# The ffn of an encoder block as seven block products for eight, with two of four sums of weights made by adding transfers

## The chip, the cores and the metric

The kernel runs on one core of a Trainium2 chip. A core has five engines that run side by side and wait for each other through semaphores: TensorE (PE, matrix products; PEld is its loading of the stationary operand), VectorE (DVE), ScalarE (ACT), GpSimd (POOL) and SyncE (SP), which here only issues transfers. Sixteen DMA engines move data between the chip's memory (HBM, "DRAM" in the code) and the core's own memory SBUF; matrix products are summed in PSUM, eight banks of 128 x 512 float32. The metric is the device time of one execution in microseconds (us), the median of the runs. The time before is 1940.48 us (three runs, 1940.22 to 1940.63).

## The reference

One block for 512 tokens of width 2048, all in float32. A norm, one input projection, two kinds of token mixing side by side, an output projection with residual; then a dense feed-forward network (ffn) with residual, and a last norm. Cut to the lines that matter here:

```
h = rmsnorm(x, norm_mix)
z = h @ w_in                                  # 2048 -> 3072
y = concat(fourier_mixer(z[:, :1024]), gating_mixer(gelu(z[:, 1024:])))
x = x + y @ w_out                             # 2048 -> 2048
h2 = rmsnorm(x, norm_ffn)
x = x + (silu(h2 @ w_gate) * (h2 @ w_up)) @ w_down     # 2048 -> 5632 -> 2048
out = rmsnorm(x, norm_final)
```

The three products of the ffn are about three quarters of all multiplications.

## The kernel before, in words

**Products.** A float32 product is made of three passes in the format float32r: each operand is split exactly into a high part and a low part, and high x high, high x low and low x high are summed in PSUM (`mm3`, lines 80 to 84). Each operand must therefore be split first. `weights` (lines 66 to 78) loads a unit of weights of 128 x 1024 (512 KB) by SP, ScalarE casts it to the high part (line 76), VectorE subtracts to get the low part (line 77). Three buffers each hold raw, high and low units, so SP's loads run up to three units ahead and wait for the buffer of an older unit.

**Stages.** The first 478 us or so make the input's norm, the Fourier half, the gate's half and the output projection. In the output projection four columns blocks of 512 (`n`) are made one after the other, each in four banks, one for each tile of 128 tokens. Behind each block VectorE adds the residual into `x2`, ScalarE makes the sums of squares, and `transposes` (lines 439 to 449) turns the block round on TensorE and splits it into `h2`. The norm's factor by token isn't known yet at that point; it is applied later, to the results of gate and up.

**The ffn.** The hidden width 5632 is 44 tiles of 128. `gate_up(f)` (lines 486 to 500) makes one tile of gate and one of up: for each, 16 steps of 128 over the width 2048, three passes each, a stationary tile of weights of 128 x 128 and 512 columns of `h2` that stream through. Then come the norm's factor, the gating (by tanh) and the split of the result, `act`. `down` (lines 505 to 511) multiplies `act` with the units of the third matrix, 512 columns wide, for a group of 4 hidden tiles at a time (`GROUPS`), and VectorE adds the result from PSUM into `x2` (line 511). Gate and up run one tile ahead of down. Behind the last small group the last norm is made and stored by token tile (lines 530 to 554).

**Order.** SP's transfers go in the order in which the code writes them. The order on the other engines is made by a planner from the dependencies, the order of the code and its own costs for each instruction: it may put an instruction forward if an earlier one isn't ready by its reckoning. On the chip each engine then works through its list in that order.

Of the kernel before, what the change touches and what calls it, by code (L numbers as in the profile page):

```python
# [38 lines left out]
def encoder_block(ctx, tc, a, out):  # L39
    """The block on one core.  # L40

    A float32 product is carried by float32r passes: an operand is hi + lo exactly, hi its
    leading 12 bits and lo the other 12, and hi*hi + hi*lo + lo*hi is accumulated in float32.
    """
# [3 lines left out]
    # loads and stores in the order written here  # L48
# [3 lines left out]
    hpool = ctx.enter_context(tc.tile_pool(name="h", bufs=2 * KT))  # L52
    spool = ctx.enter_context(tc.tile_pool(name="s", bufs=24))
# [9 lines left out]
    def htile(name):  # L63
        return hpool.tile([P, S], F32R, tag="h", name=name)

    def weights(src, name, pieces=1):
        """A unit of weights, as hi and lo."""
        raw = wpool.tile([P, U], F32, tag="raw", name=f"raw_{name}")
# [11 lines left out]
    def mm3(ps, lhs, rhs, first, last):  # L80
        """ps += lhs.T @ rhs, both as (hi, lo)."""
# [8 lines left out]
    # the tensor engine's clock rises with its use: keep it at work until the first operands are there  # L90
# [9 lines left out]
    def rsqrt(dst, ssq, scale, shape, name):  # L100
        """dst = 1 / sqrt(ssq * scale + eps), with a Newton step."""
# [22 lines left out]
    def load_h(k):  # L124
# [4 lines left out]
        hi, lo = htile(f"hhi{k}"), htile(f"hlo{k}")  # L129
# [11 lines left out]
    def by_token(pss, units, nk, lhs, name, per_k=None, then=()):  # L141
        """Four banks, one for each token tile: sum over k of lhs(k).T @ the unit's columns.
# [294 lines left out]
    h2 = []  # L437

    def transposes(n):
        for i in range(4):  # L440
# [188 lines left out]
```

## Time and profile before

| what | before |
|---|---|
| median of three runs | 1940.48 us |
| profiled execution: its span, the only time of its own that the page gives | 1938.5 us |
| TensorE busy | 1919.9 us, 99% |
| VectorE, ScalarE, GpSimd busy | 45%, 28%, 6% |
| mean granted TensorE clock | 0.997 |
| transfers | 197.51 MB, mean 102 GB/s |

The profile is one execution, recorded on the chip. Its page gives the busy time of each engine; a chain of waits, followed back from the last instruction (it tells what set the end); and groups of equal instructions with the mean time of one. Further views are asked of the same trace: busy times in chosen stretches, the chain in order of time, single instructions. Rows of groups read: line of the code, engine, operation, result and operands, shapes, count; then busy time in us, mean ns of one; then idle time of the engine before them and what ended it. Matmuls overlap in the pipeline, so the time that one really takes is the step from one start in the chain to the next, not the mean of its group. Rows of stretches read: from and to, length, busy time of PE, PEld, DVE, ACT and POOL with their instruction counts, granted clock, busy share of the DMA engines, GB/s.

### The profile page before, as it was taken

What the parts mean: (1) busy time and instruction counts of PE and PEld (TensorE: products, weight loads), DVE (VectorE), ACT (ScalarE), POOL (GpSimd) and SP (SyncE); (2) the same over time, 40 slices, a digit from 0 to 9 for tenths busy, and PEclk for the clock granted to TensorE, in tenths of its full rate; (3) what the DMA queues carried; (4) which work ended last, traced back from release to release, by engine and by line L of the source; (5) the groups of instructions that cost most, each with busy time, mean ns of one, the idle gap of its engine ahead of it and who ended that gap; (6) DMA issues with size and microseconds to landing.
All of it is one profiled execution on the core that took longest, in us unless ns stands there. A gap on an engine that the chain in (4) does not pass through costs nothing.

```text
span 1938.5 us, 20697 instructions
## 1 busy us (share of the span) xinstructions
PE 1919.9 (99%) x8610; PEld 1593.7 (82%) x8610; DVE 866.2 (45%) x1006; ACT 544.1 (28%) x684; POOL 124.2 (6%) x96
## 2 busy tenths in 40 slices
PE   9999999999999999999999999999999999999996
PEld 8888888888888888888888888888888888888885
DVE  7555663333434334343444343443433433434447
ACT  6345532223322221222212222222222122222224
POOL 5001110000000000000000000000000000000003
PEclk9999999999999999999999999999999999999998
DMA  6223224423222323323233223232232232332332
GB/s 240 95 70 108 90 74 141 142 87 119 88 98 87 109 98 98 98 91 104 89 98 98 98 87 109 87 109 98 92 100 95 94 98 98 98 98 87 106 104 94
DMA packets 55965, 197.51 MB, mean 102 GB/s; under 512 B 6592, under 2 KB 6720, under 8 KB 55872
## 3 DMA queue, kind: packets, MB, share of 16 engines
q1 hardware_dynamic: 55584, 195.15, 30.2%
q8 instruction: 67, 1.10, 0.2%
q0 software_dynamic: 288, 1.05, 0.2%
q14 instruction: 26, 0.21, 0.0%
HBM read 191.98 MB, written 4.19 MB: 101 GB/s over the span
## 4 chain that ended last, share of the span: by engine, by line
PE 97%; DVE 1%; ACT 1%; DMA 0%; issue 0%; POOL 0%; SPq 0%; ACTq 0%; DVEq 0%
PE up L83 8%; PE g L82 8%; PE g L83 8%; PE up L82 8%; PE g L84 8%; PE up L84 8%; PE d L84 8%; PE d L83 8%; PE d L82 8%; PE o L84 3%; PE o L83 3%; PE o L82 3%; PE a L82 2%; PE a L83 2%; PE a L84 2%; PE v L82 1%
## 5 line engine op out<-in xcount | busy, mean ns | idle before, releaser
L82 PE MATMUL up<-h2hi,hi_up 128*128 128x512 f32 x704 | 274.0, 389 | 0.0
L83 PE MATMUL up<-h2lo,hi_up 128*128 128x512 f32 x704 | 273.9, 389 | 0.0
L82 PE MATMUL g<-h2hi,hi_g 128*128 128x512 f32 x704 | 273.9, 389 | 0.0
L84 PE MATMUL g<-h2hi,lo_g 128*128 128x512 f32 x704 | 273.9, 389 | 0.0
L83 PE MATMUL g<-h2lo,hi_g 128*128 128x512 f32 x704 | 273.9, 389 | 0.0
L84 PE MATMUL up<-h2hi,lo_up 128*128 128x512 f32 x704 | 273.9, 389 | 0.0
L82 PE MATMUL d<-hi_d,act 128*128 128x512 f32 x672 | 261.4, 389 | 0.0
L83 PE MATMUL d<-lo_d,act 128*128 128x512 f32 x672 | 261.4, 389 | 0.0
L84 PE MATMUL d<-hi_d,act 128*128 128x512 f32 x672 | 261.4, 389 | 0.0
L511 DVE TENSOR_TENSOR x<-d,x 128x512 f32<-128x512 f32 x192 | 131.4, 687 | 160.4 <-PE d L84 159.4
L77 DVE TENSOR_TENSOR lo_up<-raw_up,hi_up 128x1024 fp32r<-128x1024 f32 x88 | 141.7, 1610 | 127.8 <-ACT hi_up L76 127.8
L76 ACT CAST hi_g<-raw_g 128x1024 fp32r<-128x1024 f32 x88 | 92.8, 1054 | 367.8 <-PE g L83 144.7
L76 ACT CAST hi_d<-raw_d 128x1024 fp32r<-128x1024 f32 x84 | 88.6, 1055 | 382.2 <-PE d L84 242.8
L77 DVE TENSOR_TENSOR lo_g<-raw_g,hi_g 128x1024 fp32r<-128x1024 f32 x88 | 107.7, 1224 | 150.7 <-ACT hi_g L76 150.6
L76 ACT CAST hi_up<-raw_up 128x1024 fp32r<-128x1024 f32 x88 | 92.8, 1054 | 272.2 <-PE up L83 140.4
L77 DVE TENSOR_TENSOR lo_d<-raw_d,hi_d 128x1024 fp32r<-128x1024 f32 x84 | 114.5, 1363 | 97.3 <-ACT hi_d L76 97.3
L84 PEld LDWEIGHTS g<-h2hi,lo_g 128*128 128x128 f32 x704 | 132.1, 188 | 27.5
L82 PEld LDWEIGHTS up<-h2hi,hi_up 128*128 128x128 f32 x704 | 132.1, 188 | 27.5
L82 PEld LDWEIGHTS g<-h2hi,hi_g 128*128 128x128 f32 x704 | 132.1, 188 | 27.4
L84 PEld LDWEIGHTS up<-h2hi,lo_up 128*128 128x128 f32 x704 | 132.1, 188 | 27.4
L83 PEld LDWEIGHTS g<-h2lo,hi_g 128*128 128x128 f32 x704 | 132.1, 188 | 27.4
L83 PEld LDWEIGHTS up<-h2lo,hi_up 128*128 128x128 f32 x704 | 132.1, 188 | 27.3
(229 smaller groups left out, 2511.6 us busy)
## 6 DMA issues: line engine op xcount, KB each, us to landing
raw_g<-in_w_gate SPq DMA_DIRECT2D x88, 512.0 KB, 3.3
raw_up<-in_w_up SPq DMA_DIRECT2D x88, 512.0 KB, 3.3
raw_d<-in_w_down SPq DMA_DIRECT2D x84, 512.0 KB, 3.3
raw_o<-in_w_out SPq DMA_DIRECT2D x32, 512.0 KB, 3.3
raw_v<-in_w_v SPq DMA_DIRECT2D x16, 512.0 KB, 3.3
raw_u<-in_w_u SPq DMA_DIRECT2D x16, 512.0 KB, 3.4
raw_a<-in_w_a SPq DMA_DIRECT2D x15, 512.0 KB, 3.5
x<-in_x SPq DMA_DIRECT2D x8, 512.0 KB, 8.0
```

Of the source, the lines that this page charges most:

```text
L76: nc.scalar.copy(hi[:, c], raw[:, c])
L77: nc.vector.tensor_sub(lo[:, c], raw[:, c], hi[:, c])
L82: mm(ps, lhs[0], rhs[0], start=first, stop=False)
L83: mm(ps, lhs[0], rhs[1], start=False, stop=False)
L84: mm(ps, lhs[1], rhs[0], start=False, stop=last)
L511: nc.vector.tensor_add(x2c(m, n), ps, x2c(m, n))
```

## The change

Strassen's scheme (in Winograd's form) makes a product of two matrices, each cut into 2 x 2 blocks, from 7 products of blocks in place of 8, with sums of blocks before and after. The change applies it once to each product of the ffn.

**Gate and up.** A block is two hidden tiles (`p` of 22) of one matrix. The seven forms of the normalised, transposed input (`hs`, four blocks and sums of them, halves of 256 tokens) are made and split once, ahead of all of them, by `ffn_input`. The norm's factor must be in the input now, so the transposes move from the output projection to behind the finished norm. Each of the seven products of a block (`product` in `matrix`) takes one unit of weights or of sums of weights, and makes 8 steps of three matmuls, 256 columns wide. Products 1 and 2 share a bank, 5 and 3 too; VectorE and ScalarE put the four results together.

**Weights.** Five raw units are loaded for a block. Two of them are sums of two quarters of the matrix: the first quarter by SP as before, the second by a transfer from GpSimd's queue that adds to what is in SBUF (`accum_op`). Two further sums are made by VectorE in `form`. Loads are written four products ahead (`LEAD`).

**Order and storage.** All of gate and up comes first. The activations, their sums and both parts of each are written to DRAM (`ad`, 512 KB a store, four for each pair of blocks, from GpSimd's queue) and are read back for down, one form of a chunk of four hidden tiles at a time. The residual goes to DRAM (`xd`) and comes back as the start of down's sums.

**Down.** Two blocks of columns (`np_`) for each group of one or two chunks; each product has `size` x 12 matmuls, 512 columns wide, in two banks; VectorE adds them into six sums, `acc`, which the last group puts together.

The buffers: `hpool` is gone, `spool` has 43 slots of 512 KB for 24, the three high and low buffers stay.

```
-GROUPS = [4] * 10 + [2, 2]
+GROUPS = [2, 2, 2, 2, 2, 1]
+FORMS = 7
...
+            if n % 2:
+                nc.gpsimd.dma_start(xd[m, n // 2], x2[m][n // 2])
...
+    ORDER = (1, 5, 2, 6, 7, 3, 4)
+        LOADS = ((1, 0, (0,)), (5, 1, (0, 1)), (2, 2, (2,)), (3, 3, (3,)), (7, 4, (3, 1)))
...
+    def load_raw(r, i, srcs, name):
+        r[i] = slot(f"raw{i}_{name}")
+        nc.sync.dma_start(r[i], srcs[0])
+        for more in srcs[1:]:
+            nc.gpsimd.dma_start(r[i], more, accum_op=ALU.add)
...
+    def form(r, i, name):
...
+        elif i == 6:
+            nc.vector.tensor_add(r[5], r[5], r[3])
+        w = split_weights(r[5] if i in (6, 4) else r[i], f"{name}_{i}")
+        if i == 6:
+            nc.vector.tensor_add(r[5], r[5], r[2])
+        return w
...
+    def combine(t, A11, A12, A21, A22):
+        nc.vector.tensor_sub(t[0], A21, A22)
+        nc.vector.tensor_sub(t[1], t[0], A11)
+        nc.vector.tensor_add(t[2], t[1], A12)
+        nc.vector.tensor_sub(t[3], A11, A21)
+
+    def ffn_input(n):
+        xn = [slot(f"xn{n}_{i}", F32, (P, 2, S)) for i in range(2)]
+        for m in range(NT):
+            nc.vector.tensor_scalar_mul(xn[m // 2][:, m % 2, :], x2c(m, n), rstd2[:, m : m + 1])
+        r = [slot(f"h2_{n}_{i}", F32, (P, 2, S)) for i in range(2)]
+        for i in range(4):
...
+            for m in range(NT):
+                nc.tensor.transpose(ps[:, m * P : (m + 1) * P], xn[m // 2][:, m % 2, i * P : (i + 1) * P], ident)
+            nc.scalar.mul(r[i // 2][:, i % 2, :], ps, g_ffn[:, c : c + 1])
...
+        combine(t, A11, A12, A21, A22)
+        for i, s in ((1, A11), (5, t[0]), (2, A12), (6, t[1]), (7, t[3]), (3, t[2]), (4, A22)):
+            x = slot(f"hs{n}_{i}", F32R, (P, 2, 2, H))
+            nc.scalar.copy(x[:, :, 0, :], s)
+            nc.vector.tensor_sub(x[:, :, 1, :], s, x[:, :, 0, :])
+            hs[n][i] = x
...
+        def product(i, into, first=True):
+            step()
+            hi, lo = form(r, i, name)
...
+            for j in range(KT // 2):
+                x = hs[j // 2][i][:, j % 2]
...
+                mm(b, lo[:, c], x[:, 0, :], start=first and j == 0, stop=False, skip_group_check=True)
...
+                    mm(b, hi[:, c], x[:, 1, :], start=False, stop=False, skip_group_check=True)
+                    mm(b, hi[:, c], x[:, 0, :], start=False, stop=last, skip_group_check=True)
+            return b
+        A = product(1, "A")
+        nc.scalar.copy(m1, A)
+        E5 = product(5, "D")
+        A = product(2, "A", False)
+        nc.scalar.copy(o[:, 0, 0, :], A)
+        B = product(6, "B")
+        nc.vector.tensor_add(u, B, m1)
+        C = product(7, "C")
+        nc.vector.tensor_add(w, C, u)
+        nc.vector.tensor_sub(o[:, 1, 1, :], E5, w)
+        E5 = product(3, "D", False)
+        nc.vector.tensor_sub(o[:, 1, 0, :], E5, u)
+        E = product(4, "E")
+        nc.vector.tensor_add(o[:, 0, 1, :], E, w)
+        return o
...
+    def activation(p, g, u):
+        s = slot(f"s{p}", F32, (P, 2, 2, H))
+        nc.scalar.activation(s, g, AF.Tanh, scale=0.5)
+        nc.vector.scalar_tensor_tensor(s, s, 1.0, g, op0=ALU.add, op1=ALU.mult)
+        nc.vector.scalar_tensor_tensor(s, s, 0.5, u, op0=ALU.mult, op1=ALU.mult)
+        t = slot(f"at{p}", F32, (P, 4, H))
+        combine([t[:, i, :] for i in range(4)], s[:, 0, 0, :], s[:, 1, 0, :], s[:, 0, 1, :], s[:, 1, 1, :])
+        to = ad[p // 2].rearrange("f p r l h -> p f r l h")
+        for i, src in enumerate((s.rearrange("p a b c -> p (a b) c"), t)):
...
+            nc.scalar.copy(hi, src)
+            nc.vector.tensor_sub(lo, src, hi)
+            nc.gpsimd.dma_start(to[:, 4 * i : 4 * i + 4, p % 2, 0, :].bitcast(F32), hi.bitcast(F32))
+            nc.gpsimd.dma_start(to[:, 4 * i : 4 * i + 4, p % 2, 1, :].bitcast(F32), lo.bitcast(F32))
...
+    LEAD = 4
...
+    def step():
+        for args in wanted.pop(steps[0] + LEAD, ()):
+            load_raw(*args)
+        steps[0] += 1
...
+    def load_acts(i, chunk, size):
+        for c in range(chunk, chunk + size):
+            t = acts[c, i] = slot(f"a{c}_{i}", F32R, (P, 2, 2, H))
+            nc.sync.dma_start(t.bitcast(F32), ad[c, PLACE[i]].bitcast(F32))
...
+    def down(b):
...
+        def product(i, into, begin=True):
+            step()
...
+            for q in range(size):
+                hi, lo = form(r[q], i, f"{name}_{q}")
...
+                        mm(ps[into][t], xh, hi[:, c], start=start, stop=False, skip_group_check=True)
+                        mm(ps[into][t], xh, lo[:, c], start=False, stop=False, skip_group_check=True)
+                        mm(ps[into][t], xl, hi[:, c], start=False, stop=stop, skip_group_check=True)
+            if np_ == 1 and gi + 1 < len(GROUPS):
+                load_acts(i, chunk + size, GROUPS[gi + 1])
...
+        add("u", product(1, "A"), first)
+        add(22, product(5, "D"))
+        add(11, product(2, "A", False))
...
```

What is left out of the matmuls' loops in `down` runs over two halves of the chunk and two token tiles of 128. In the last group `down` also puts the sums together and squares them; the last norm's scaling of 16 tiles and the stores follow behind all of it.

More of the change, by code (lines that the diff above doesn't have):

```diff
@@ L427, in encoder_block @@
     x2 = [[slot(f"x2_{m}_{i}") for i in range(2)] for m in range(NT)]
+    xd = dram.tile([NT, 2, P, U], F32, name="xd")
     def load_x(i):
@@ L465, in encoder_block @@
     rsqrt(rstd2, xs, 1.0 / D, [P, NT], "ffn")
[L466 to L477 removed]
+    hs = [dict() for _ in range(4)]
@@ L530, in encoder_block @@
-    for n in range(4):
-        raw = wpool.tile([P, U], F32, tag="raw", name=f"raw_l{n}")
-        nc.sync.dma_start(raw, a["w_down"][f0 // 2][n])
-        p = pair(f"dl{n}")
-        split(raw, p)
-        units.append([p])
-    for m in range(NT):
-        o = [slot(f"o{m}_{i}") for i in range(2)]
-        oc = [o[n // 2][:, (n % 2) * S : (n % 2 + 1) * S] for n in range(4)]
-        for n in range(4):
-            down(f0, size, m, n, units[n], bank(f"d{f0}_{m}_{n}"))
-            squares(m, n, fss[:, m, n : n + 1])
-            last = m == NT - 1 and n == 3
-            (nc.vector if last else nc.gpsimd).tensor_tensor(
-                out=oc[n], in0=x2c(m, n), in1=gB[n // 2][:, (n % 2) * S : (n % 2 + 1) * S], op=ALU.mult
-            )
+    acts = {}
@@ L546, in encoder_block @@
+    for i in ORDER:
+        load_acts(i, 0, GROUPS[0])
+    for b in range(2 * FP, len(blocks)):
+        _, _, (gi, chunk, size, np_) = blocks[b]
+        down(b)
+        if np_ == 0 and gi == len(GROUPS) - 1:
+            for i in range(2):
+                nc.sync.dma_start(gB[i], a["norm_final"][:, i * U : (i + 1) * U].partition_broadcast(P))
+    for m in (0, 1, 2, 3):
+        half, t = m // 2, m % 2
         r = fr[:, m : m + 1]
```

231 lines of the change are left out of this document (150 added, 81 removed).

## The prediction

> **What bounds the kernel now.** I read the page's busy times first, then the chain of waits, then the busy times by stretches, then single rows for the price of each operation.
>
> ```profile
> span 1938.5 us, 20697 instructions
> PE 1919.9 (99%) x8610; PEld 1593.7 (82%) x8610; DVE 866.2 (45%) x1006; ACT 544.1 (28%) x684; POOL 124.2 (6%) x96
> PE 97%; DVE 1%; ACT 1%; DMA 0%; issue 0%; POOL 0%; SPq 0%; ACTq 0%; DVEq 0%
> 485.60:1923.00 1437.40, 1437.25 (x6344) 1189.71 (x6342) 613.76 (x662) 343.82 (x388) 71.58 (x56) 1.00 0.29 96
> 12.00:22.00 10.00, 10.00 (x46) 8.29 (x45) 10.00 (x7) 9.46 (x15) 9.61 (x6) 1.00 0.98 378
> 1903.59 0.23 PE d L84
> ...
> 1910.16 0.23 PE d L83
> ```
>
> TensorE is the bound: 97% of the chain, and through the ffn (485.6 to 1923) it is never idle, at full clock, with DVE 43% busy and the DMA engines at 0.29. Only fewer or shorter matmuls can help, while everything else has half its time to spare. The last row of stretches (columns: PE, PEld, DVE, ACT, POOL, clock, DMA share, GB/s) is the start, where transfers queue: full DMA engines carry 378 GB/s here. The two chain rows are 29 steps of the 128x512 matmul apart: 6.57/29 = 0.2266 us each; the 6336 of the ffn make 1436 us.
>
> **What it removes.** Seven block products for eight. Down goes from 2112 matmuls of 512 columns to 1848, at 0.2266: 478.6 to 418.8, so 60 us less. Gate and up go from 4224 of 512 columns (957.2 us) to 44 blocks x 7 products x 24 = 7392 of 256 columns. Their price stands in the Fourier stage:
>
> ```profile
> 119.06 0.12 PE dft L82
> ...
> 119.77 0.06 PE dft L82
> 119.83 0.12 PE dft L83
> ...
> 120.39 0.17 PE E L82
> ```
>
> The six matmuls from 119.06 to 119.77 are 256 wide: 0.1183 each. The five from 119.83 to 120.39 are 128 wide: 0.112, so there is a floor just below, where the load of weights sets the pace. I take 0.1185: 7392 x 0.1185 = 876 us, a gain of 81 and not the 120 of an eighth. A product then lasts 2.84 us, a block 19.9, 44 blocks 876. Bounds: 0.1170 and 0.125, 865 to 924.
>
> **The head.** Now three of the four transposes (1.88 us each) stand between output products, and TensorE goes from the fourth straight into the gate. After the change all wait for the finished norm, then for normalising, transposing, sums and splits of seven forms.
>
> ```profile
> 483.68 1.88 PE xt L444 x16
> 490.84 0.16 DVE L115 TENSOR_SCALAR rstd<-rsq_ffn 128x4 f32<-128x4 f32 x1
> L204 DVE TENSOR_SCALAR a0a<-a0a,rstd 128x512 f32<-128x512 f32 x2 | 0.9, 482 | 0.0
> L459 DVE TENSOR_TENSOR x<-o,x 128x512 f32<-128x512 f32 x16 | 10.9, 692 | 4.4 <-PE o L84 4.4
> ```
>
> The output products end at 483.7 - 3 x 1.88 = 478.0. The norm is ready 491.0 - 483.7 = 7.3 later: 485.3. Then VectorE does, for each of four column groups, 4 scalings of 0.482, 4 sums and 7 low parts of 512 elements at 0.692: 9.5, in all 38.2 us. Product 1 needs the fourth group's first form, behind which six low parts (4.2) are left: 519.3. TensorE can by then have done three quarters of products 1 and 5 (4.3 us, their banks are separate), so gate and up begin, in effect, at 515.0. If the planner takes one form of all groups first, some 8 us earlier (507); if TensorE does nothing meanwhile, 519.
>
> **VectorE's load.**
>
> ```profile
> L77 DVE TENSOR_TENSOR lo_g<-raw_g,hi_g 128x1024 fp32r<-128x1024 f32 x88 | 107.7, 1224 | 150.7 <-ACT hi_g L76 150.6
> L376 DVE SCALAR_TENSOR_TENSOR vn_lo<-v,vr,vn_hi 128x1024 fp32r<-128x1024 f32 x4 | 5.0, 1279 | 1.2 <-ACT vn_hi L375 1.2
> L511 DVE TENSOR_TENSOR x<-d,x 128x512 f32<-128x512 f32 x192 | 131.4, 687 | 160.4 <-PE d L84 159.4
> L253 DVE TENSOR_TENSOR ey<-ey,O 128x128 f32<-128x128 f32 x16 | 6.1, 379 | 0.0
> L76 ACT CAST hi_g<-raw_g 128x1024 fp32r<-128x1024 f32 x88 | 92.8, 1054 | 367.8 <-PE g L83 144.7
> ```
>
> A gate or up block: 7 low parts and 2 sums of weights at 1.224 (11.0); 5 sums from PSUM, 256 wide, not in the trace, between 0.379 (128 wide) and 0.687 (512), by the line through 0.69 and 1.22 nearer the lower: 0.43 to 0.48 (2.3); half an activation, which is two combined operations of 1.279, four sums of 0.43 and two low parts, 6.7 (3.4). Together 16.7 of 19.9 us: 84% busy, beside work that TensorE hides. A down block of two chunks lasts 7 x 24 x 0.2266 = 38.1 and gives VectorE 18 x 1.224 + 14 x 0.687 = 31.6, 83%. ScalarE has 7 casts of 1.054, two small copies and half an activation, under 10 of 19.9. VectorE has cover, but little.
>
> **Waits that it adds.** Each is bounded from nothing (covered) to its full length; all 57 us of them are estimates.
> - In a gate or up block product 3 adds into bank D, which product 5 filled and which `o[1,1]` must read first, behind `w`, behind product 7. Two 256-wide sums, 0.9, and up to a split of 1.2 ahead of them: 0 to 2.1 a block, 0 to 92. Product 4 has its own bank and can cover it if the planner puts it forward. It does such things:
>
> ```profile
> 496.47 0.44 PE rstd2B L475 x4
> 496.91 0.24 PE up L82
> 497.15 0.64 PE rstd2B L475 x4
> ```
>
> Here four broadcasts stood ready, four did not, and an up product was put between, though the code writes all eight first. I take 0.5 a block, 22.
> - Behind each pair of blocks VectorE has sum, combination, four sums and two low parts, 5.9 us, and the two products split ahead (three buffers) last 5.7; the next split is late by 0 to 2.0. I take 1.0 x 22 = 22. The activation's four stores queue on POOL ahead of the adding transfers of the next block, which so wait for it too.
> - Last group, one chunk: VectorE has 9 x 1.224 + 14 x 0.687 + 4 x 1.224 = 25.5 a block, TensorE 19.0: 0 to 13 over the two, I take 8.
> - Down's first product waits behind the residual's 4.2 MB and the first form's activations (1.0 MB) on SP's queue, which need slots that the last up block frees: 5.2 MB at 378 GB/s is 13.8. I take 5, of 0 to 14.
>
> **The tail.**
>
> ```profile
> 1922.46 0.39 PE L84 MATMUL d<-dl_hi,act 128*128 128x512 f32 x1
> 1930.57 0.16 DVE L547 TENSOR_REDUCE fs<-fss 128x1 f32<-128x4 f32 x1
> ...
> 1931.88 0.15 DVE L115 TENSOR_SCALAR fr<-rsq_fin 128x1 f32<-128x1 f32 x1
> L389 DVE SCALAR_TENSOR_TENSOR v<-sv,g_sgu,bB 128x512 f32<-128x512 f32 x8 | 5.9, 747 | 2.2 <-PE sv L84 2.2
> out_dram<-o SPq DMA_DIRECT2D x16, 256.0 KB, 2.8
> ```
>
> Now 1938.5 - 1922.9 = 15.6. After: two sums and a square (2.2), four token tiles at 1.46 for the norm and 4 x 0.747 = 3.0 for the scaling (17.8; no tile has all its squares before the last block), issue and landing (3.4): 23, of which a tile's start fits under the last product: 22.
>
> **The sum**, against the execution's own span: 515 + 876 + 419 + 22 = 1832, with the waits' 57 1889. The page gives the profiled execution no time but its span; the median of the runs, 1940.48, is 2.0 above it. So 1891.
>
> **The transfers.** Gate and up read 7 units of 512 KB a block for 4 and write 2 units of activations: 4.72 MB in 19.9 us, 237 GB/s. Down reads, in two blocks, 28 units of weights and 14 of activations: 22.0 MB in 76.2 us, 289 GB/s. Both are under 378, so I cost them at nothing: the cover is the spare third of the DMA engines.
>
> ```profile
> raw_g<-in_w_gate SPq DMA_DIRECT2D x88, 512.0 KB, 3.3
> wsp<-in_w_spatial POOLq DMA_DIRECT2D x1, 512.0 KB, 4.0
> L306 POOL DMA_DIRECT2D wsp<-in_w_spatial x1 | 0.7, 720 | 0.0
> L77 DVE TENSOR_TENSOR lo_up<-raw_up,hi_up x88: 1212/1225/2302, 484.9 to 1863.9; 128x1024 fp32r<-128x1024 f32 x88
> ```
>
> But two of the seven add to what lies in SBUF, and no transfer here adds. Say one occupies the engines like m plain ones: m = 1 from below (a plain POOL load lands in 4.0 against SP's 3.3), m = 4 from above if it were as far off as 4.0 x 4. At 1.387 us a unit a block needs (7 + 2m) units, a down pair 34 + 8m. I take m under 2.6, where both still fit. The Trainium skill ("Collectives: The Full Stack", "The bandwidth ceiling: the fold count and why AG ≠ RS ≠ AR") says that an adding transfer is slower because it reads two sources, about half the rate of a copy. That would be m = 2, a down pair at 69 of 76 us, and the sum as it is; no run here shows it.
>
> Other edits at nothing: the residual's 8 stores of 512 KB on POOL's queue fall where POOL has no arithmetic (the output products), the final norm's weights, now loaded a block before the end, are wanted only in the tail, and 22 x 4 activation stores are in the 2 units a block. If that cover were gone, a store costs its unit, 1.387 us.
>
> **Rivals.**
> - **The adding transfers pace it** (slower): with m = 4 a block needs 15 x 1.387 = 20.8 us for 19.9 (+40 over 44), a down pair 91.6 for 76.2 (+85 over 5.5). With half the waits (they fall under these) 1832 + 28 + 125 + 2 = 1987. It decides against the change from m of about 3.7. For it: lead of four products, 11.4 us, must hold a load, the adding and the split, 3.3 + 4.0 + 2.3 at idle queues. Against: spare a third, and a factor of 4 has no row. 0.21.
> - **VectorE paces it.** The last row quoted shows a split of 1.2 us held up to 2.3 when POOL works. If the four POOL transfers a block hold it for 0.72 each, 16.7 + 2.9 = 19.6, and 0.1 at each of 16 hand-overs makes 21.2: 44 x 1.3 = 57 in place of the first two waits' 44, so 1904; with down likewise near its 38.1, up to 1925. POOL computes nothing more in the ffn, which speaks against. The Trainium skill ("SBUF — State Buffer", "Who interferes with whom") says a VectorE operation with two SBUF inputs collides with POOL's reads, and infers that making descriptors needs the write side only; by that this rival falls. 0.18.
> - **The planner hides nearly all**: waits near 10 and the head at 507: 1836. 0.13.
> - **It isn't fewer cycles**: 256-wide matmuls in a long stream cost 0.1295, where gate and up gain nothing (957 / 7392): 1891 + 81 = 1972. The rows have six in a row, hardly slower than half. 0.04.
>
> **How the numbers follow.** Forecast 0.44, its own range 1850 to 1925. Low 1835 is the planner's case, high 1990 the adding transfers'. Under 0.2% (3.9 us) a measurement of this kernel tells nothing. Faster: 0.44 + 0.13 + 0.17 = 0.74; slower: 0.20 + 0.03 + 0.01 = 0.24; same 0.02.
>
> **What would show it.** TensorE at 0.1185 per 256-wide matmul; from the last output product to steady gate work some 37 us; a gate block of about 21 us, with the gap ahead of product 3 and behind each up block; down blocks near 38.5; a tail of 22. Wrong if the gaps end on raw tiles (transfers, m), if VectorE shows above 95% in gate and up, or if product 3's gap is over 1 us.

## The result, and the profile after

The changed kernel takes 2317.7 us (median of four runs, 2313.7 to 2321.7), the kernel before 1940.35 us beside it (1940.0 to 1940.6). The ratio is 1.1945, with a 95% interval of 1.1928 to 1.1962: 377 us slower, where 1891 us, 49 us faster, was predicted, and outside the predicted range. The profiled execution spans 2317.6 us against the predicted 1889.

The page of the changed kernel: span, busy times, granted clock in 40 slices, transfers of GpSimd's queue (q0), and the chain by engine and by line.

```profile
span 2317.6 us, 28514 instructions
PE 1929.6 (83%) x11506; PEld 1741.3 (75%) x11506; DVE 1304.8 (56%) x1577; ACT 799.7 (35%) x976; POOL 236.0 (10%) x265
PEclk9997788899979988888898899888888889999998
q0 software_dynamic: 33120, 120.60, 21.8%
PE 55%; DMA 11%; DVE 9%; issue 4%; ACT 3%; POOL 2%; POOLq 0%; DVEq 0%; ACTq 0%; SPq 0%
```

TensorE, 97% of the chain before, is 55% of it. No other engine took its place as the bound: VectorE is at 56%, the transfers at 11% of the chain. The kernel waits, now here and now there, and the clock falls with it. Where it waits is told by the busy times in stretches (columns as before: PE, PEld, VectorE, ScalarE, GpSimd, clock, DMA share, GB/s):

```profile
106.00:206.00 100.00, 76.88 (x377) 62.96 (x375) 38.99 (x98) 36.42 (x62) 6.26 (x6) 0.88 0.24 75
206.00:300.00 94.00, 60.81 (x231) 47.69 (x232) 36.20 (x42) 33.26 (x45) 6.48 (x5) 0.78 0.12 37
300.00:484.00 184.00, 140.22 (x583) 111.15 (x582) 54.03 (x66) 34.47 (x43) 8.85 (x7) 0.87 0.36 130
665.80:1850.60 1184.80, 975.27 (x7394) 965.71 (x7392) 682.48 (x792) 410.13 (x469) 143.47 (x173) 0.89 0.62 180
1852.50:2295.00 442.50, 427.04 (x1848) 349.97 (x1848) 342.55 (x368) 172.11 (x181) 39.27 (x46) 0.98 0.84 267
```

The first three rows lie ahead of the ffn, where no product was changed, and TensorE stands idle a quarter of the time there. The fourth is gate and up: 210 us idle, and a clock of 0.89. The last is down, 16 us above the predicted 427. The waits of TensorE that cost most (total, times, longest):

```profile
PE C_gate L559 <- DVE lo_gate L481: 149.9, 22, 10.1
PE u L82 <- ACT hi_u L76: 62.9, 8, 21.3
PE B_gate L559 <- DVE lo_gate L481: 59.6, 21, 3.0
PE xt L525 <- DVE xn L519: 30.2, 4, 8.2
PE v L82 <- ACT hi_v L76: 25.0, 3, 15.4
```

Set against the terms of the prediction, with the repaired kernel of the last experiment (called the repaired head there) beside it; each number is the distance between single rows of TensorE's timeline:

| term | predicted | changed kernel | repaired head |
|---|---|---|---|
| output products end at | 478.0 | 621.1 | 479.0 |
| from there to the first gate matmul | 37 | 44.7 | 23.3 |
| gate and up | 876 + 44 of waits | 1184.8 | 911.6 |
| gap ahead of down | 5 | 1.9 | 2.3 |
| down | 419 + 8 | 442.6 | 447.3 |
| tail | 22 | 22.5 | 23.5 |
| span | 1889 | 2317.6 | 1887.0 |

Of the 429 us missed, 143 lie ahead of the ffn, 8 in the head (from the output products to the first gate matmul), 265 in gate and up, 16 in down; the gap ahead of down was 3 shorter.

**What each gap waits for.** Ahead of the ffn TensorE waits for casts of `u` and `v`, and these for loads. Before, SP's queue waited there almost only for the split that empties one of the kernel's own three raw buffers (`SPq L73 <- DVE lo_o L77: 155.2, 30, 6.9`, and likewise for the other matrices; no wait for an operation of the mixing is above 5.9 us). In the changed kernel the loads of the same units wait for slots that other work holds:

```profile
SPq L73 <- ACT vt L365: 83.6, 5, 51.9
SPq L73 <- DVE yg L171: 62.2, 4, 39.7
```

The diff turned the three raw buffers and the 32 halves for `h` into ordinary slots of one pool of 43. A weight unit that was loaded into a buffer of its own now waits for a slot of a result of the gating half.

In gate and up, one pair of blocks lasts some 54 us. GpSimd's timeline around one of the gaps ahead of `C_gate` (product 7 of gate):

```profile
1200.79 0.80 POOL L598 DMA_DIRECT2D ad<-ahi  x1 [28.82 <-ACT ahi L596]
1204.45 0.79 POOL L599 DMA_DIRECT2D ad<-alo  x1 [2.86 <-DVE alo L597]
1205.23 0.75 POOL L598 DMA_DIRECT2D ad<-ahi  x1
1206.72 0.75 POOL L599 DMA_DIRECT2D ad<-alo  x1 [0.74 <-DVE alo L597]
1207.46 0.96 POOL L475 DMA_DIRECT2D raw_gate<-in_w_gate  x1
```

The adding transfer for product 7 waits for nothing of its own. Its plain load was issued by SP at 1187.69 and had long landed (the loads of gate take 12.8 us at most); the adding transfer stands behind four stores that wait for the activation, 28.8 us for the first of them. From there the chain in order of time:

```profile
1207.46 10.24 DMA raw_gate<-in_w_gate
...
1217.78 1.05 ACT hi_gate L480
...
1218.86 1.24 DVE lo_gate L481
...
1220.14 0.58 PE C_gate L559
...
1223.50 0.21 PE C_gate L564
...
1223.92 0.15 PE C_gate L563
...
1224.18 0.12 PE C_gate L559
```

Landing takes 10.2 us, with the DMA engines full meanwhile (a share of 1.05 from 1212.9 to 1220.1, against 0.62 on average in gate and up), then cast and split, and only then product 7. After an idle time of 7.3 us its first 17 matmuls take 3.8 us, most of them 0.21 each and not 0.12: the granted clock is 0.50 from 1220.2 to 1223.7 and 1.00 from 1224 on. That is a second cost of the same gap. Over all of gate and up it comes to 88 us: TensorE is busy for 975.3 us, and 7392 matmuls at 0.12 would be 887. By the steps, 54 of it follow gaps ahead of product 7 and 33 gaps ahead of product 6 (`B_gate`).

### The profile page after: what moved, and what is told of

It reads as the page before. It is cut to its first block, busy times and chain, and to the rows that moved or that the text cites. A ratio compares the mean times of both kernels' runs of the same rounds, so it can differ in the third digit from the quotient of the medians.

```text
span 2317.6 us, 28514 instructions
## 1 busy us (share of the span) xinstructions
PE 1929.6 (83%) x11506; PEld 1741.3 (75%) x11506; DVE 1304.8 (56%) x1577; ACT 799.7 (35%) x976; POOL 236.0 (10%) x265
## 3 DMA queue, kind: packets, MB, share of 16 engines
q0 software_dynamic: 33120, 120.60, 21.8%
## 4 chain that ended last, share of the span: by engine, by line
PE 55%; DMA 11%; DVE 9%; issue 4%; ACT 3%; POOL 2%; POOLq 0%; DVEq 0%; ACTq 0%; SPq 0%
DMA raw_gate<-in_w_gate 9%; PE o L82 2%; PE o L83 2%; PE o L84 2%; DVE lo_gate L481 2%; ACT hi_gate L480 2%; PE D_up L559 2%; PE C_gate L559 2%; PE D_up L564 2%; PE A_up L564 2%; PE A_up L559 2%; PE A_up L563 2%; PE D_up L563 2%; PE A_d L691 2%; PE A_d L692 2%
## 5 line engine op out<-in xcount | busy, mean ns | idle before, releaser
L480 ACT CAST hi_gate<-raw_gate 128x1024 fp32r<-128x1024 f32 x154 | 154.9, 1044 | 298.9 <-DMA raw_gate<-in_w_gate 140.4
L481 DVE TENSOR_TENSOR lo_gate<-raw_gate,hi_gate 128x1024 fp32r<-128x1024 f32 x154 | 184.1, 1219 | 122.2 <-ACT hi_gate L480 122.2
L481 DVE TENSOR_TENSOR lo_up<-raw_up,hi_up 128x1024 fp32r<-128x1024 f32 x154 | 188.5, 1224 | 101.6 <-ACT hi_up L480 101.2
L559 PE MATMUL C_gate<-hs,lo_gate 128*128 128x256 f32 x176 | 73.7, 419 | 149.9 <-DVE lo_gate L481 149.9
L559 PE MATMUL A_gate<-hs,lo_gate 128*128 128x256 f32 x352 | 111.3, 316 | 0.0
L82 PE MATMUL u<-h,hi_u 128*128 128x512 f32 x128 | 58.8, 459 | 62.9 <-ACT hi_u L76 62.9
L563 PE MATMUL A_gate<-hs,hi_gate 128*128 128x256 f32 x352 | 110.5, 314 | 0.0
L564 PE MATMUL A_gate<-hs,hi_gate 128*128 128x256 f32 x352 | 109.9, 312 | 0.0
L559 PE MATMUL B_gate<-hs,lo_gate 128*128 128x256 f32 x176 | 54.9, 312 | 59.6 <-DVE lo_gate L481 59.6
L77 DVE TENSOR_TENSOR lo_o<-raw_o,hi_o 128x1024 fp32r<-128x1024 f32 x32 | 39.0, 1224 | 112.5 <-ACT hi_o L76 112.5
L559 PE MATMUL D_up<-hs,lo_up 128*128 128x256 f32 x352 | 101.5, 288 | 0.0
L559 PE MATMUL D_gate<-hs,lo_gate 128*128 128x256 f32 x352 | 100.2, 285 | 0.0
L564 PE MATMUL A_up<-hs,hi_up 128*128 128x256 f32 x352 | 99.6, 283 | 0.0
L559 PE MATMUL A_up<-hs,lo_up 128*128 128x256 f32 x352 | 99.6, 283 | 0.0
L563 PE MATMUL A_up<-hs,hi_up 128*128 128x256 f32 x352 | 99.6, 283 | 0.0
L563 PE MATMUL D_gate<-hs,hi_gate 128*128 128x256 f32 x352 | 99.6, 283 | 0.0
L564 PE MATMUL D_up<-hs,hi_up 128*128 128x256 f32 x352 | 99.5, 283 | 0.0
## 6 DMA issues: line engine op xcount, KB each, us to landing
raw_up<-in_w_up POOLq DMA_DIRECT2D x44, 512.0 KB, 12.8
```

Source lines behind the costliest of these rows:

```text
L77: nc.vector.tensor_sub(lo[:, c], raw[:, c], hi[:, c])
L82: mm(ps, lhs[0], rhs[0], start=first, stop=False)
L480: nc.scalar.copy(hi, raw)
L481: nc.vector.tensor_sub(lo, raw, hi)
L559: mm(b, lo[:, c], x[:, 0, :], start=first and j == 0, stop=False, skip_group_check=True)
L563: mm(b, hi[:, c], x[:, 1, :], start=False, stop=False, skip_group_check=True)
```

## The experiments

The theory: three unrelated delays, none of them a slow operation. Slots shared with the stages ahead of the ffn (143 us); adding transfers behind stores on GpSimd's queue (150 us, and the clock with it); splits behind the activation's work on VectorE (60 us, and the clock). Its rivals are those of the prediction: the adding transfers are dear in themselves, or VectorE has too much to do. Beside these runs the kernel before took 1940.4 to 1941.2 us.

### Raw buffers of their own, ahead of the ffn

```diff
-    spool = ctx.enter_context(tc.tile_pool(name="s", bufs=43))
+    spool = ctx.enter_context(tc.tile_pool(name="s", bufs=40))
-        raw = slot(f"raw_{name}")
+        raw = wpool.tile([P, U], F32, tag="raw", name=f"raw_{name}")
```

> The changed kernel, but the weights of all stages ahead of the ffn are loaded into three raw buffers of their own again, as in the kernel before, and the shared pool has 40 slots for 43. Theory 1 (storage: in the changed kernel SP's loads ahead of the ffn wait for slots of the shared pool, which results of mixing hold): the output products end at about 480 us for 626, TensorE is idle there by under 10 us in all, and the whole is about 2317 - 145 = 2170, with gate and up as long as before, 1186. Rival 1 (something else slows the first part, the stores of the residual or the clock): the output products end at 600 or later, the whole within 20 us of 2317.

2246.9 us. Two of the stretches, and the wait that grew:

```profile
106.00:206.00 100.00, 100.00 (x509) 84.83 (x508) 53.61 (x108) 43.46 (x68) 6.38 (x6) 1.00 0.31 94
206.00:300.00 94.00, 92.79 (x458) 78.30 (x457) 57.89 (x76) 43.66 (x61) 14.18 (x11) 1.00 0.27 85
```

```profile
PE C_gate L559 <- DVE lo_gate L481: 213.0, 22, 13.5
```

Ahead of the ffn the loss is gone: full clock, and the output products end at 479.8, within 2 us of the predicted 478.0. That shows the storage as the cause of the 143 us. The whole gained only 71, for in the ffn the wait for product 7 rose from 149.9 to 213.0. All that the edit changes there is the number of slots, 40 for 43; how that makes the wait longer was not followed further. The gain was right in its place and the expectation wrong for the whole.

### The kernel before, with shared slots

```diff
-    hpool = ctx.enter_context(tc.tile_pool(name="h", bufs=2 * KT))
-    spool = ctx.enter_context(tc.tile_pool(name="s", bufs=24))
+    spool = ctx.enter_context(tc.tile_pool(name="s", bufs=43))
-        raw = wpool.tile([P, U], F32, tag="raw", name=f"raw_{name}")
+        raw = slot(f"raw_{name}")
```

(`h`, `h2` and down's raw units likewise from slots.)

> The kernel before with one edit: raw weights and the split inputs of gate, up and the projections share one pool of 43 slots, as in the changed kernel; the bytes are the same. Theory 1 (storage): the stages ahead of the ffn take 105 to 145 us longer, and the ffn, which holds few other tiles, little, so 2045 to 2090. Rival 1: within 10 us of 1940, and the loss of the first part comes from elsewhere in the change.

2589.8 us, 500 more than expected. The waits:

```profile
PE g L78 <- ACT hi_g L72: 128.7, 34, 4.7
PE up L78 <- ACT hi_up L72: 105.7, 44, 3.4
PE u L78 <- ACT hi_u L72: 62.7, 8, 21.3
```

The stages ahead lost some 160 us, with the wait for `u` as in the changed kernel (62.7 against 62.9): sharing alone does it, with no Strassen in the kernel. But the ffn before also starved, which I had not expected: gate and up wait for casts, the casts for loads that wait for slots. Why it lost so much more there (some 490 us, of which TensorE's named waits are 234 in these two rows) was not taken apart further.

### A lead of five products for four

```diff
-    LEAD = 4
+    LEAD = 5
```

> The changed kernel with loads written five products ahead for four. On POOL's queue the adding transfer for product 7 of a gate block then stands ahead of the four activation stores of the pair of blocks before, not behind them. Theory 2 (head of line: that transfer waits for VectorE's low parts of activations, not for the DMA engines): TensorE's wait ahead of product 7 of gate (149.9 us in 22) falls under 20, the slow matmuls behind it go with it, and the whole is 2317 - 22 x (7 + 1.6) = about 2130. Rival 2 (slots or the transfer itself are late whatever the order): the wait moves to another product, and the whole stays within 60 us of 2317.

2126.2 us, 191 less, as expected. `C_gate` no longer waits; the wait for `B_gate` stays:

```profile
PE B_gate L559 <- DVE lo_gate L481: 59.8, 21, 3.1
```

The wait was 149.9 us and 191 were won. The rest fits the slow steps behind these gaps, 54 us in the changed kernel, of which other waits take some back (down's first, `A_d`, grew from 1.9 to 14.4). With five, the adding transfers for the next gate come ahead of the stores on GpSimd's queue (in the pair looked at they are issued at 1182.49 and 1192.87, the next store at 1209.78). But every load also starts a product, 2.9 us, earlier. Two more runs, further down, were made to part the two.

### Plain transfers for adding ones

```diff
-            nc.gpsimd.dma_start(r[i], more, accum_op=ALU.add)
+            nc.gpsimd.dma_start(r[i], more)
```

> The changed kernel with the two adding transfers of a block as plain ones that overwrite, on the same queue and in the same order; it leaves out the sums of two of the four weights' sums, so its output isn't the block's. It measures what adding costs by itself. If adding occupies the DMA engines twice (m = 2) or more and that delays TensorE, the whole falls by over 100 us and the time from issue to landing of POOL's loads (8.0 and 12.8 us) falls to SP's 4 to 9. Theory 2 (order of the queue): TensorE's wait ahead of product 7 of gate stays within 40 us of 149.9, and the whole within 60 us of 2317.

2279.4 us, 38 less.

```profile
q0 software_dynamic: 33120, 120.60, 14.3%
PE C_gate L559 <- DVE lo_gate L481: 119.4, 22, 8.6
```

This prices the adding itself: 21.8% of 2317.6 us less 14.3% of 2277.6 is 180 us of all engines in 132 transfers, 1.36 us each. A plain unit on that queue takes 1.45: 14.3% of 2277.6 is 326 us, of which the 98 stores and other transfers are 135 (the run with sums on VectorE, below, has these alone on the queue: 5.8% of 2328.6), and the rest falls on 132. So m = 1.94. (The stores-from-ScalarE run below, with almost nothing but adding transfers on the queue, gives 18.1% of 2197.7 us, some 2.9 each, which agrees.) The rival, m near 4, falls, and with it the idea that the adding paces gate and up: at half its price the wait for `C_gate` shrinks by a fifth.

### Stores written later in the code, and stores from ScalarE

The first of the two kernels only writes the four stores behind the load of product 7:

```diff
-            nc.gpsimd.dma_start(to[:, 4 * i : 4 * i + 4, p % 2, 0, :].bitcast(F32), hi.bitcast(F32))
+            late.append((to[:, 4 * i : 4 * i + 4, p % 2, 0, :].bitcast(F32), hi.bitcast(F32)))
...
             load_raw(*args)
+        while late:
+            nc.gpsimd.dma_start(*late.pop(0))
```

> The changed kernel with one thing moved: the four activation stores of a pair of blocks are issued from GpSimd's queue behind the adding transfer for product 7 of the next gate block, not ahead of it. The lead of all loads stays four products and every load keeps its place on SP's queue. If what delays product 7 of gate is the order on GpSimd's queue, its wait (149.9 us in 22) all but goes, B_gate's 59.6 stays, and the time falls as it did with a lead of five: by 150 to 195, to 2123 to 2168. If it was the lead (a load, an adding transfer and a split don't fit into four products) and the queue's order is beside the point, C_gate keeps at least two thirds of its wait and the time stays above 2260.

2315.7 us, and `C_gate` waits 149.9 us as ever. It doesn't tell the two apart: in the trace GpSimd's queue has the same order as before, the last store and then the adding transfer. The planner put the stores first all the same.

```profile
1205.59 0.75 POOL L631 DMA_DIRECT2D ad<-alo  x1 [0.74 <-DVE alo L597]
1206.33 0.96 POOL L475 DMA_DIRECT2D raw_gate<-in_w_gate  x1
```

The second kernel takes the stores off the queue:

```diff
-            nc.gpsimd.dma_start(to[:, 4 * i : 4 * i + 4, p % 2, 0, :].bitcast(F32), hi.bitcast(F32))
+            nc.scalar.dma_start(to[:, 4 * i : 4 * i + 4, p % 2, 0, :].bitcast(F32), hi.bitcast(F32))
```

> The changed kernel with the four activation stores of a pair of blocks issued by ScalarE, which makes or waits next to what they store; GpSimd's queue holds the adding transfers alone, in the order that they had. The lead stays four products. If the adding transfer for product 7 of gate is late because it stands behind stores that wait for the activation, it now starts when its plain load has landed, some 14 us earlier, C_gate's wait (149.9 us in 22) falls below 15, B_gate's 59.6 stays or grows by what ScalarE's stores hold up (4 issues of under 0.1 us and the wait for the last low part, up to 2 us a pair, 0 to 44), and the time falls by 130 to 195, to 2122 to 2188. If what counts is the lead, C_gate keeps two thirds of its wait and the time stays above 2260.

2199.5 us. The waits:

```profile
PE B_gate L559 <- DVE lo_gate L481: 83.6, 21, 4.2
...
PE A_d L690 <- DMA a<-ad: 26.0, 1, 26.0
...
PE C_gate L559 <- DVE lo_gate L481: 1.7, 1, 1.7
```

With the lead still at four, `C_gate` waits 1.7 us in all. So the queue's order is the cause, and the lead is long enough. The 118 us won are less than the 130 to 195 expected: `B_gate`'s wait grew by 24 us, which the expectation allowed for, and down's first wait by 24, which it did not.

### Work in the gap

56 matmuls of 256 columns into a bank that nobody reads, ahead of product 7 of each gate block but the first.

```diff
+        if name.startswith("gate") and name != "gate0":
+            fb = bank(f"fill_{name}")
+            for n in range(56):
+                mm(fb[:, :H], hs[0][1].bitcast(F32R)[:, 0, 0, :P], hs[0][1][:, 0, 0, :], start=True, stop=True)
         C = product(7, "C")
```

> The changed kernel with 56 matmuls into a bank that nobody reads, written between products 6 and 7 of each gate block but the first (21 blocks), 56 x 0.118 = 6.6 us, where TensorE waits some 7. Theory 4 (TensorE's clock falls after some us of idling, so that the 17 matmuls behind the wait take 0.213 us each for 0.118): product 7's matmuls are at 0.118 from the start, the time falls by 21 x 17 x 0.095 = 34 less what the filling overruns the wait by (under 15). Rival 4 (their operands come late, not the clock): the matmuls of product 7 stay at 0.213 and the time doesn't fall.

2283.6 us: 34 less, with 1176 matmuls more. Groups of product 7 (min, median and max of the recorded time in ns; first and last start), in the changed kernel, then with the filling:

```profile
L563 PE MATMUL C_gate<-hs,hi_gate x176: 274/415/420, 680.2 to 1824.0; 128*128 128x256 f32 x176
```

```profile
L563 PE MATMUL C_gate<-hs,hi_gate x176: 278/283/416, 681.6 to 1790.2; 128*128 128x256 f32 x176
```

The gap is a little longer than it was (21 x 6.7 us of filling and 19.4 of waits left, for 149.9), but TensorE is idle for an eighth of it, and product 7 runs at full clock but for a few blocks. By the steps, the slow matmuls behind the gaps cost 9 us in place of 54; the filling overruns the waits by some 11. So idling costs a second time, here at least 34 / 21 = 1.6 us a gap, and it is the idling that does it: a matmul that nobody needs is cheaper than none.

### Sums of weights on VectorE

```diff
-    if True:
+    if False:
         LOADS = ((1, 0, (0,)), (5, 1, (0, 1)), (2, 2, (2,)), (3, 3, (3,)), (7, 4, (3, 1)))
...
-        if i == 5 and not True:
+        if i == 5:
```

> The changed kernel with all four sums of weights on VectorE and no adding transfers (four quarters loaded plainly). By theory 2 the 150 us of waits ahead of product 7 of gate go, since no load stands behind the activation stores on POOL; VectorE has 16.7 + 2.4 = 19.1 of 19.9 us a block and adds waits of its own, 0.5 to 2 us a block, so 2317 - 185 + 22 to 88 = 2150 to 2220. If the adding transfers were the better way even so, it is slower than 2317.

2330.4 us, a miss: no adding transfer is left, and nothing is won. The waits of `C_gate` and `B_gate` are gone from the list, as expected, but others of the same size have come. The waits, and most of gate and up:

```profile
PE D_gate L559 <- DVE lo_gate L481: 162.7, 22, 7.4
...
PE D_up L559 <- DVE lo_up L481: 58.7, 22, 2.8
```

```profile
700.00:1800.00 1100.00, 896.90 (x6767) 888.16 (x6768) 738.10 (x806) 375.83 (x424) 60.21 (x80) 0.88 0.34 115
```

VectorE is busy for 67% of the time and still late: product 5 stands second in a block, and its sums and its split queue behind the activation of the pair before. In the pair looked at, product 5's sum starts only when the activation's work of 1211.7 to 1217.9 is done. That speaks for VectorE's order and against its load, though no run here changes that order alone: what was late behind GpSimd's queue is now late behind VectorE's.

### Both repairs, then VectorE's burst spread

Raw buffers of their own (also for the units of products 1 and 7 of the ffn) and a lead of five; then, beside that, the activation's low parts, sums and stores no longer in one go but in pieces behind products 5, 6 and 7 of the next block:

```diff
+            if pieces:
+                pieces.pop(0)()
...
+        pieces.extend([
+            lambda: None,
+            lambda: store(0, s.rearrange("p a b c -> p (a b) c")),
+            lambda: None,
+            sums,
+            lambda: store(1, t[0]),
+        ])
```

> Both repairs in one: three raw buffers of their own (used ahead of the ffn for all weights, in the ffn for the raw units of products 1 and 7), 40 shared slots, and loads written five products ahead. If the two causes are independent, 2126 - 142 = about 1984, with the output products ending at 480 and TensorE's wait ahead of product 7 of gate gone. If the shared pool is too small in gate and up once three slots are tied to two of the five units, waits on raw units come back there and it stays above 2030.

> The same with the activation's low parts, sums and stores written piece by piece behind products 5, 6 and 7 of the next block, so that VectorE makes the split for product 6 ahead of the sums. Theory 3 (the wait ahead of product 6 of gate, 59.8 us in 21, is VectorE's burst of activation work): that wait falls under 10, the slow matmuls behind it go, 16 x 0.095 us x 21 = 32, and the whole is 1984 - 60 - 32 = about 1895, faster than the kernel before. Rival 3 (that split is late because its raw sums are, by transfers): the wait stays, the whole stays within 20 us of the run without the pieces.

1995.1 us, then 1906.9 (four runs, 1905.7 to 1908.0; ratio to the kernel before 0.9826, 0.9810 to 0.9842). The first is 11 above the sum of the two repairs; 10 of it is down's first wait, `A_d`, 24.5 us here and 14.4 with the lead of five alone. Gate and up with the burst spread, and what is left of waits there:

```profile
530.00:1450.00 920.00, 894.19 (x7355) 887.35 (x7353) 681.82 (x796) 414.29 (x463) 147.94 (x177) 0.99 0.79 233
```

```profile
PE A_d L711 <- DMA a<-ad: 24.2, 1, 24.2
```

`B_gate`'s wait was 54.3 us and spreading won 88: again the wait, and about 34 of clock (21 gaps at 1.6). The pieces move the stores on GpSimd's queue too; for VectorE as the cause speaks also that in the changed kernel it is busy for the whole 3.06 us from 1202.24 to 1205.30, one of these gaps. With the storage, the queue and the burst repaired, and the same arithmetic, the scheme takes 1.7% less time than the kernel before. VectorE does the same work, 682 us, in 920 us where it had 1185.

### Sums on VectorE in the repaired kernel

The edit of the sums on VectorE, on top of the spread kernel; the raw buffers of their own serve product 1 alone.

> The repaired kernel (own raw buffers, here for product 1 alone, five products ahead, activation by pieces) with all four sums of weights on VectorE and no adding transfers. It tells what the adding transfers are worth once nothing else stands in the way. Theory: VectorE has 16.7 + 2.4 = 19.1 of 19.9 us a block in gate and up, and in down 22 x 1.224 + 14 x 0.687 = 36.5 of 38.1, so it paces both, with 0.5 to 2 us of TensorE's waits a block: 1907 + 22 to 88 = 1929 to 1995. Rival: the adding transfers buy nothing, within 10 us of 1907 or below.

2117.4 us, ratio 1.0914 (1.0898 to 1.0930), against 1929 to 1995 expected.

```profile
PE D_gate L564 <- DVE lo_gate L484: 82.2, 22, 6.4
PE D_up L564 <- DVE lo_up L484: 58.7, 22, 2.8
```

A miss of the same kind as the first. With the activation spread, product 5's sums still queue behind sums of results that wait for TensorE; that this is all of it was read from the trace and not tried. So without its adding transfers, the suspect of the prediction, the repaired kernel is 210 us slower (the use of the raw buffers differs a little too).

### Down's first activations, and the head

In the spread kernel 5.2 MB stood on SP's queue ahead of down's first product. The first run loads each form's activations first and puts the residual's parts between them. The second also scales all of `x2` in place, ahead of the transposes, where before each column group's scaling was written behind the last group's sums and splits:

```diff
+    for i, k in zip(ORDER, (None, 22, 11, None, 12, 21, None)):
+        load_acts(i, 0, GROUPS[0])
+        if k:
+            load_residual(k, 0)
```

```diff
+    for n in range(4):
+        for m in range(NT):
+            nc.vector.tensor_scalar_mul(x2c(m, n), x2c(m, n), rstd2[:, m : m + 1])
...
-        xn = [slot(f"xn{n}_{i}", F32, (P, 2, S)) for i in range(2)]
```

> The repaired kernel with the loads at the start of down in the order of their use: two activations, then the residual's part that is added first, and so on, in place of all 4.2 MB of residual first. If down's first product waits (24.2 us) for its activations because they stand behind the residual on SP's queue, the wait falls by 10 to 17 and the whole to about 1893. If it waits for slots that the last up block frees, the whole stays within 5 us of 1907.

> The same, and all sixteen scalings by the norm's factor, in place in the residual's tiles, ahead of the first low part on VectorE. In the changed kernel the scaling of a column group stands on VectorE behind the seven low parts of the group before, so TensorE's transposes and all that follows come in four steps of 11.9 us. If that is why the head lasts 46 us and not the 37 of the prediction, it falls by 8 to 10 and the whole to about 1884. If the transposes at TensorE's low clock set it, it falls by under 3.

1902.2 us, then 1888.8 (four runs, 1888.7 to 1890.6; ratio 0.9738, 0.9722 to 0.9754). The first won less than 5 us, a third of what was expected. By its size that is the expectation's other case, that down waits for slots; the trace shows the order at work too, for `A_d`'s wait fell from 24.2 to 2.3 us, and a new one came, `PE B_d L708 <- DMA a<-ad: 10.4, 1, 10.4`. What sets the rest is open. The second won 13.4 us more, where 8 to 10 was expected. The head, in the chain of the spread kernel and then of the last one:

```profile
484.40 0.50 DVE xn L522
...
484.95 3.87 PE xt L528 x16
...
492.19 4.21 DVE hs L538 x7
...
496.40 0.41 DVE xn L522
```

```profile
484.46 6.42 DVE x L652 x16
...
493.42 4.21 DVE hs L535 x7
...
500.16 3.01 DVE hs L535 x5
```

In the first a group takes 11.9 us (484.40 to 496.40 is 12.0): scaling, transposing and splitting in turn, with VectorE idle during the transposes, because the next group's scaling is queued behind the seven low parts. The 16 transposes of a group take 3.87 us there, for 1.88 in the kernel before: between 626.5 and 662 in the changed kernel the granted clock is 0.60. In the second VectorE does all scalings first and goes from one group's splits to the next with no gap, 6.7 us a group. It beats both kernels of the case. That its span of 1887.0 lies 2 us from the predicted one is luck: by the table the head is 14 us shorter than predicted, gate and up 8 shorter and down 20 longer.

## Why the prediction was wrong, step by step

**The step that is missing: the storage of the other stages (143 us).** The prediction prices every edit of the ffn and takes the output products' end, 478.0, from the trace of before, as if what lies ahead of the ffn could not change. The diff's line on the buffers was described and never costed. The kernel with own raw buffers gives the 143 us back in place, and the kernel before loses some 160 there when its slots are shared. Among "other edits at nothing" it should have stood as one that has a cover: SP's three raw buffers, and what it costs if they are gone.

**The step that was mis-sized: GpSimd's queue (1.0 us a pair predicted for it and the burst together).** The text had the mechanism: "The activation's four stores queue on POOL ahead of the adding transfers of the next block, which so wait for it too". It priced it inside the 22 us of the burst. It cost 149.9 us of waits, 6.8 a pair, and 191 in all, with the clock. The error was to count what the burst delays VectorE and not what a transfer that starts late still has ahead of it: 10.2 us to land, a cast, a split, with product 7 wanted meanwhile. The sentence in the rivals, a lead of 11.4 us that must hold a load, the adding and a split, presumed that the adding starts when its load has landed. It started 19.8 us after the load was issued. The cover that the transfers were given, a spare third of the DMA engines, is an average: in the gap shown the engines were full while the late transfer landed.

**The burst on VectorE: 1.0 us a pair predicted, 59.6 / 22 = 2.7 measured in the changed kernel,** and 88 us in all with the clock, where spreading it took it away. Right in kind.

**The clock: not in the prediction.** It used 0.1185 for each matmul, at full clock. In the changed kernel the slow matmuls behind the two gaps of a pair cost 88 us (975.3 us busy for 887). Two runs measured such a part: 34 us of filled gaps ahead of product 7, and 34 (88 less 54) of the spread burst.

**Bank D: 22 predicted, nothing measured.** No wait of `D_gate` or `D_up` stands in the changed kernel's list. The planner puts `E_gate`, which has a bank of its own, ahead, as the prediction had held possible.

**The head: 37 predicted, 44.7 measured.** VectorE was taken as busy throughout. It stood idle for 13.4 us in four waits for the transposed blocks: TensorE could transpose only what had been scaled (its own four waits for that are 30.2 us), and the scalings were in line behind the splits of the group before.

**Right.** The step of a 256-wide matmul: 0.12 against 0.1185 (7392 x 0.0015 is 11 us). Down: 442.6 against 427 with its waits. The tail: 22.5 against 22. Of the rivals, "the adding transfers pace it" came nearest by its sum, 1987, and was wrong by its cause: m was measured at 1.94, under the 2.6 assumed. The Trainium skill's "Collectives: The Full Stack" ("The bandwidth ceiling: the fold count and why AG ≠ RS ≠ AR") has ReduceScatter at half the rate of a copy because the add needs two source reads; for the adding into SBUF here the trace agrees with that page. By the prediction's own signs, gaps that end on raw tiles meant transfers and m. They did end on raw tiles, and it was not m: the sign could not tell a transfer that is slow from one that starts late. "VectorE paces it" falls by its load, 58% of gate and up, where 84% of a block of 19.9 us had been reckoned (682 / 44 is 15.5 us a block, predicted 16.7). "Not fewer cycles" falls by the 0.12.

## What to carry to other kernels

A transfer that needs nothing but a free queue is late by whatever its queue waits for: before transfers move to another engine's queue, list what stands ahead of them there and what each of these waits for, and read the order from the engine's timeline and not from the code. A pool of buffers that takes in those of another stage changes that stage too; price it there, even if no line of its work has changed. A mean share of busy DMA engines is no cover for a transfer that comes late and is wanted at once. And give each wait of TensorE of some three microseconds or more its second price, matmuls behind it at half the clock.

## What the runs showed of the hardware

- Behind an idle gap of TensorE of 7.3 us, matmuls of 256 columns step 0.213 us until 3.8 us after its end, at a granted clock of 0.50, then 0.12. Behind the other gaps ahead of `C_gate` in the changed kernel, of 5.1 to 10.1 us, such a stretch has 13 to 28 slow matmuls, 2.7 to 5.9 us. Shorter gaps can do it too, but not each of them. Of 20 gaps ahead of `B_gate`, all of 2.93 to 3.02 us, 4 were followed by no such stretch, 11 by one of 13 to 16 slow matmuls and 5 by one of 26 to 28; gaps of 0.84, 1.74 and 1.94 us were followed by none. Nor need it begin at once: in the pair shown a gap of 2.93 us ended at 1205.34, and the steps of 0.21 went from 1206.76 to 1210.13. What else than its length decides what follows a gap is not shown here.
- The Trainium skill ("TensorE: Matmul & The Clock Gate", "What's actually happening") has half the clock, 1.2 GHz, after an idle window of about 3.4 us, and the full clock again after a busy window of about 3.4 us. At N / 1.2 ns a matmul, which the same page gives for the slow state under "Wait — 56ns, not 53.3ns?", 256 columns would take an estimated 213 ns. The trace agrees with the step; the slow stretches here last 2.7 to 5.9 us, and in 16 of the 20 cases a gap shorter than the page's, 2.93 to 3.02 us, was enough.
- An adding transfer of 512 KB into SBUF occupies the DMA engines 1.36 us longer than a plain one of 1.45, 1.94 times as much, and VectorE's splits beside them keep their 1.22 us.
